# Operands moved ahead in the hand-placed front of a hybrid encoder layer

## The chip, the cores and the metric

One core of a Trainium2 chip runs the whole kernel. The metric is device time in microseconds of one execution, and the figure for a kernel is the median of its runs. TensorE (PE), VectorE (DVE), ScalarE (ACT), GpSimd (POOL) and SyncE (SP) each execute their own instructions in order; most DMAs are issued by SP, some by POOL, and they share 16 DMA engines.

## The reference, cut to what matters

One encoder layer on 1024 tokens of width 1024, float32:

```
h   = LN(x)
q, k, v, g, u, aq, ak, av = split(h @ W_in)      # 2048 columns
ret = silu(g) * groupnorm(retention(q, k, v))    # 4 heads of 64, chunks of 128
s5  = gated(C . scan(lam_bar, B u) + D u)        # 16 groups, 16 channels, 64 complex states, both directions
att = windowed GQA with ALiBi and a sink logit   # 8 heads of 64, 2 key heads, window 128
h   = LN(alpha*h + concat(ret, s5, att) @ W_out)
out = LN(alpha*h + expert_choice_swiglu(h))      # 16 experts, 128 tokens each, width 2048
```

Every float32 weight of the big products is split on the chip into a high and a low float32r part; each product is then three matmuls (high by high, high by low, low by high).

## The kernel before

`build` has three stages. `front` writes its steps into a `Plan`: `at(place, step)` gives each step a place on one axis, and `run` emits the steps sorted by place, so that the order on every engine and on SP's DMA queue is the order of the places. Places are an order, not times. After `front` a middle stage (attention scores and outputs, output projection, first layer norm, router) is emitted in a loop over half tiles and its order on the engines is chosen by the framework's scheduler. The experts, again in a written order, stream 384 pieces of weights of 1 MB.

`front` in order: eight token tiles are normalized (`Norm`: load, stats, gain, shift, turn, parts) and projected to retention keys and values (`Project`). The logarithms of the decays, `retention_consts`, are a chain of some 20 small GpSimd operations that begins with four on DVE; `decays`, on ACT, needs its end. `Norm.stats` uses GpSimd too, for one power. Then comes the S5 input product `up` (`Turned`, into `s5_input`), the input operators (`inputs`, DVE; `inputs_turn`, PE; `inputs_put`, ACT) and the output operators (`outputs`, DVE; `outputs_store`, SP: `wo_dram`; two buffers `work`). The input `u` is stored by channel to `ut_dram` and loaded by step as `U` (eight DMAs of 512-byte pieces, in the same buffer as `uT`); `s5_states_part` multiplies it with the operators, eight times, and ACT and DVE copy real and imaginary parts into `VS`. The scan (`s5_scan`, `s5_carry`) runs on DVE between other steps, and `s5_states_store` writes the states out.

`Lags` makes the short convolution blocks `m_dram`, in eight parts on PE, each with two loads (`WO`, `BX`) on SP; `Lags.store` writes one group's blocks in eight DMAs on SP. The rest of the projections runs in the order of the string `order` (`K`, `V`, `q`: attention; `g`: retention gates; `r`: retention chunks; `o`: S5 outputs). The weights of the last two query units, `W7`, are loaded at `where["r5"]`.

The output stage `Output` has four products `o0` to `o3`. Each needs a tile `MUW` of 128x4x4x128 float32 (1.05 MB: lags' blocks, `u`, two output operators; four DMAs) and two tiles `Z` of states (0.26 MB each). Their space, pool `s5o`, opens at place `O`, when the retention buffers close, so all the loads stand behind it on SP, with four buffers of `MUW`. Between them stand twelve stores of attention queries (`q_d`, 0.13 MB each) and the loads of `w_out` (`Matrix.load`, four of 1.05 MB through two `raw` buffers; `parts` splits them on ACT and DVE). `put` applies Gelu on ACT behind `parts` of the same step; `turn`, `gate` and `gated` follow and `store` writes `y2_dram`. As the last retention matrices leave, GpSimd loads the attention keys and values (3.1 MB).

The middle stage begins with `attention_consts` (distances and sinks), the loads of the layer norm's rows, `router_weights` and the first `out_proj_load`, which needs `y2_dram`.

Of the kernel before, what the change touches and what calls it, by code (L numbers as in the profile page):

```python
# [439 lines left out]
class Params:  # L440
# [4 lines left out]
    def __init__(self, K, I, pool, work):  # L445
# [12 lines left out]
        K.LT = K.s5small.tile([P, 2, 16, 16], F32, name="LT")  # L458
        K.A = K.s5small.tile([P, 2, 2, 2, 16], F32, name="A")
# [167 lines left out]
def s5_input(K, p, m, half):  # L627

    if m == 0 and half == 0:
        K.uT = K.s5w.tile([P, 2, 8, P], F32, name="uT", tag="U")  # L630
    K.nc.scalar.activation(K.uT[:, m, :, half * 64:(half + 1) * 64], p.ps.rearrange("p (k j) -> p j k", j=8), AF.Copy)


def s5_input_store(K, m):
    K.nc.sync.dma_start(K.ut_dram[m * P:(m + 1) * P], K.uT[:, m])


def s5_input_load(K):
# [74 lines left out]
class Lags:  # L713
# [35 lines left out]
    def store(self, g2):  # L749
# [5 lines left out]
        for j in range(8):  # L755
            nc.sync.dma_start(K.m_dram[g2][j * 16:(j + 1) * 16],
# [3 lines left out]
class Output:  # L760
# [17 lines left out]
    def load(self, g2, q):  # L778
# [3 lines left out]
        x = self.pool.tile([P, 4, 4, P], F32, name="MUW", bufs=4)  # L782
# [158 lines left out]
def front(K, I, pool, close):  # L941
# [35 lines left out]
    spread(4.5, 0.01, ops[4:])  # L977
# [4 lines left out]
    at(8.1, lambda: WK[0].high(1))  # L982
# [119 lines left out]
    for i, (d, q, g2) in enumerate((d, q, g2) for d in range(2) for q in range(2) for g2 in range(2)):  # L1102
# [5 lines left out]

    steps, blocks = s5_scan(K)
# [7 lines left out]
    at(e2 + 1.0, lambda: close(X["s5v"][0]))  # L1117
# [24 lines left out]
    X["out"] = Output(K, I)  # L1142
    out = X["out"]
    qs = [(g2, q) for g2 in range(2) for q in range(2)]
    for w in order:
        where[w] = s
        if w[0] in "KVq":
# [22 lines left out]
        elif w[0] == "r":  # L1170
# [12 lines left out]
            at(s + 12, c.store)  # L1183
# [13 lines left out]
    for wt, place, prev in ((W6, V0 + 15, ("K1", "V1")), (W7, where["r5"], ("q01", "q11"))):  # L1197
# [15 lines left out]
    for i, k in enumerate(qs):  # L1213
        at(O + 0.1 + 0.1 * i if i < 2 else O + 0.3 + 0.1 * i, lambda k=k: out.load(*k))
# [869 lines left out]
def build(tc, nc, I, O):  # L2084
# [193 lines left out]
```

## Time and profile before

| what | value |
|---|---|
| median of 3 runs | 1725.3 us (1721.63 to 1726.28) |
| the profiled execution, its own time | 1729.55 us |
| its span, first to last instruction | 1727.8 us |
| mean granted TensorE clock | 0.977 |
| PE busy | 1613.1 us, 93% |
| DVE busy | 1413.4 us, 82% |
| ACT busy | 1123.5 us, 65% |
| POOL busy | 203.1 us, 12% |
| moved by DMA | 512.83 MB, 297 GB/s |

Busy time is that of instructions on the engine; a busy PE is not PE at its peak, since the ends of matmuls are modelled. The clock is the granted share of 2.4 GHz. Times in rows are microseconds from the span's start.

### The profile page before, as it was taken

What the parts mean: (1) busy time and instruction counts of PE and PEld (TensorE: products, weight loads), DVE (VectorE), ACT (ScalarE), POOL (GpSimd) and SP (SyncE); (2) the same over time, 40 slices, a digit from 0 to 9 for tenths busy, and PEclk for the clock granted to TensorE, in tenths of its full rate; (3) what the DMA queues carried; (4) which work ended last, traced back from release to release, by engine and by line L of the source; (5) the groups of instructions that cost most, each with busy time, mean ns of one, the idle gap of its engine ahead of it and who ended that gap; (6) DMA issues with size and microseconds to landing.
All of it is one profiled execution on the core that took longest, in us unless ns stands there. A gap on an engine that the chain in (4) does not pass through costs nothing.

```text
span 1727.8 us, 21181 instructions
## 1 busy us (share of the span) xinstructions
PE 1613.1 (93%) x7748; PEld 1301.5 (75%) x7748; DVE 1413.4 (82%) x1721; ACT 1123.5 (65%) x1249; POOL 203.1 (12%) x235
## 2 busy tenths in 40 slices
PE   6988988489999899999999999999999999999996
PEld 4866877377777678888888888888888777777775
DVE  6886773257677998988888889898898999999995
ACT  4634353267654667777777777777777777877773
POOL 3000011001101001001011010010110313221121
PEclk9999999789999999999999999999999999999998
DMA  4564458732313899999999999999999999999993
GB/s 174 188 142 115 130 162 235 242 118 74 99 49 116 320 358 378 389 401 374 380 387 365 387 361 372 398 358 387 375 378 398 386 390 402 378 421 374 378 386 147
DMA packets 114475, 512.83 MB, mean 297 GB/s; under 512 B 13121, under 2 KB 40513, under 8 KB 63554
## 3 DMA queue, kind: packets, MB, share of 16 engines
q1 hardware_dynamic: 104242, 481.58, 73.8%
q0 software_dynamic: 10128, 29.89, 5.6%
q8 instruction: 61, 1.00, 0.2%
q14 instruction: 44, 0.36, 0.1%
HBM read 464.24 MB, written 47.19 MB: 296 GB/s over the span
## 4 chain that ended last, share of the span: by engine, by line
PE 59%; DVE 12%; DMA 11%; issue 7%; ACT 5%; SPq 3%; POOL 1%; POOLq 0%; DVEq 0%; ACTq 0%
PE gu L1753 25%; PE y L1753 12%; DVE whl L1800 6%; PE mm L74 4%; PE mm L76 4%; PE mm L75 4%; DMA zz<-acc_d 3%; DMA wraw<-in_exp_w_up 3%; DMA wraw<-in_exp_w_down 2%; ACT whl L1793 2%; PE tp L1738 2%; PE tp L1303 1%; SPq L787 1%; SPq L895 1%; DMA wraw<-in_w_out 1%
## 5 line engine op out<-in xcount | busy, mean ns | idle before, releaser
L1800 DVE TENSOR_TENSOR whl<-wraw,whl 128x2048 fp32r<-128x2048 f32 x384 | 873.5, 2289 | 101.2 <-ACT whl L1793 101.1
L1793 ACT ACTIVATE whl<-wraw 128x2048 fp32r<-128x2048 f32 x384 | 734.9, 1917 | 245.8 <-PE gu L1753 77.7
L1753 PE MATMUL gu<-whl,xT 128*128 128x512 f32 x3072 | 738.2, 397 | 0.0
L1753 PEld LDWEIGHTS gu<-whl,xT 128*128 128x128 f32 x3072 | 569.7, 188 | 123.9
L1753 PE MATMUL y<-whl,hT 128*128 128x512 f32 x1536 | 368.7, 395 | 0.7 <-ACT hT L65 0.7
L1753 PEld LDWEIGHTS y<-whl,hT 128*128 128x128 f32 x1536 | 288.7, 188 | 69.4 <-ACT hT L65 0.9
L1727 POOL DMA_INDIRECT xs<-h_d,index x15 | 41.4, 2757 | 740.8 <-PE y L1753 488.5
L74 PE MATMUL mm<-hT,whl 128*128 128x512 f32 x160 | 67.2, 420 | 4.9 <-ACT gate L354 3.3
L65 ACT ACTIVATE hT<-tp 128x512 fp32r<-128x512 f32 x80 | 46.1, 584 | 30.0 <-PE tp L1738 15.2
L76 PE MATMUL mm<-hT,whl 128*128 128x512 f32 x160 | 64.6, 403 | 0.0
L75 PE MATMUL mm<-hT,whl 128*128 128x512 f32 x160 | 64.4, 403 | 0.0
L66 DVE TENSOR_TENSOR hT<-tp,hT 128x512 fp32r<-128x512 f32 x80 | 54.2, 684 | 6.8 <-ACT hT L65 6.8
L1738 PE MATMUL tp<-ident,hid 128*128 128x128 f32 x256 | 39.6, 278 | 18.5 <-DVE hid L1835 18.5
L1738 PEld LDWEIGHTS tp<-ident,hid 128*128 128x128 f32 x256 | 31.1, 142 | 31.0 <-DVE hid L1835 24.2
L74 PE MATMUL mm<-WO,yh 128*128 128x512 f32 x128 | 52.8, 412 | 1.6 <-ACT yh L65 1.5
L75 PE MATMUL mm<-WO,yh 128*128 128x512 f32 x128 | 51.3, 401 | 0.0
L1283 ACT ACTIVATE S<-S,asm 128x384 f32<-128x384 f32 (+1 forms) x64 | 36.9, 578 | 21.3 <-DVE asm L1279 21.3
L1276 DVE CUSTOM_DVE_ANT_0 S<-at,R,sink 128x384 f32<-128x384 f32 (+1 forms) x64 | 35.8, 579 | 17.7 <-PE at L1274 13.7
L76 PE MATMUL mm<-WO,yl 128*128 128x512 f32 x128 | 50.3, 402 | 0.0
L74 PE MATMUL mm<-whl,hT 128*128 128x512 f32 (+1 forms) x128 | 47.6, 372 | 1.6 <-DVE kst L889 1.2
L1835 DVE TENSOR_TENSOR hid<-hid,gu 128x512 f32<-128x512 f32 x64 | 43.6, 681 | 1.8 <-PE gu L1753 1.8
L76 PE MATMUL mm<-whl,hT 128*128 128x512 f32 (+1 forms) x128 | 44.5, 347 | 0.0
(432 smaller groups left out, 1815.2 us busy)
## 6 DMA issues: line engine op xcount, KB each, us to landing
wraw<-in_exp_w_gate SPq DMA_DIRECT2D x128, 1024.0 KB, 8.0
wraw<-in_exp_w_up SPq DMA_DIRECT2D x128, 1024.0 KB, 8.0
wraw<-in_exp_w_down SPq DMA_DIRECT2D x128, 1024.0 KB, 7.8
wraw<-in_w_in SPq DMA_DIRECT2D x8, 1024.0 KB, 7.2
x<-in_x SPq DMA_DIRECT2D x8, 512.0 KB, 4.5
h_d<-x SPq DMA_DIRECT2D x8, 512.0 KB, 3.1
q_d<-kst SPq DMA_DIRECT2D x32, 128.0 KB, 3.2
qs<-q_d POOLq DMA_DIRECT2D x16, 256.0 KB, 3.4
```

The lines of the kernel that those rows point to most:

```text
L65: nc.scalar.activation(hi, src, AF.Copy)
L66: eng.tensor_tensor(lo, src, hi.bitcast(F32), OP.subtract)
L74: nc.tensor.matmul(ps, a[0], b[0], start=start, stop=False)
L75: nc.tensor.matmul(ps, a[0], b[1], start=False, stop=False)
L76: nc.tensor.matmul(ps, a[1], b[0], start=False, stop=stop)
L1283: nc.scalar.activation(S[g][:, :W], S[g][:, :W], AF.Exp, bias=nm[:, g:g + 1], accum_out=rs[:, g:g + 1])
L1727: nc.gpsimd.indirect_dma_start(out=xs, out_offset=None, in_=K.h1_dram, in_offset=bass.IndirectOffsetOnAxis(ap=K.index[:, e:e + 1], axis=0))
L1738: K.nc.tensor.transpose(pt[:, c, :], src[:, (c0 + c) * P:(c0 + c + 1) * P], K.ident)
L1753: nc.tensor.matmul(ps, a[s][c], u[:, t, i * w:(i + 1) * w], start=first and id(ps) not in began, stop=last and left[id(ps)] == 0)
L1793: self.K.nc.scalar.activation(u[:, 0, :], self.raw[k1].rearrange("p a b -> p (a b)"), AF.Copy)
L1800: self.K.nc.vector.tensor_tensor(u[:, 1, :], raw, u[:, 0, :].bitcast(F32), OP.subtract)
L1835: at(self.after, q, 3, lambda: nc.vector.tensor_tensor(self.h[q], self.h[q], self.pg[q][1], OP.mult))
```

## The change

The start: the decay logits are the first load; the GpSimd chain (`ops[4:]`) moves behind the second tile's statistics; the second tile's gain and shift move ahead of the second weight unit's split, and half of the first tile's product ahead of the second tile's turn. The `inputs_turn` steps are spread, the first earlier, the others later. `uT` becomes a tile of its own and is stored by step straight to `u_dram` (eight stores of 64 KB for each half `m`), `U` is read back in two DMAs, `ut_dram` and the store of `U` go; the state parts run half by half. The copies into `VS` write in order and read PSUM with a step of 16 elements, instead of the reverse. The lags' blocks are stored from GpSimd's queue. `W7` is loaded some 50 places earlier. As the scan's space closes, two new pools open in it: `early` (attention's constants, the router's operands) and `s5m` (the first two `MUW` and the first `Z` pair), and the router's weights are made there. `s5o` keeps two `MUW` buffers. The first two loads of `w_out` move ahead by 4.6 places, some stores by 2 places, and the first two expert weights are issued inside the middle loop, at its step 9.

```diff
@@ Params.__init__
+        K.uT = pool.tile([P, 2, 8, P], F32, name="uT")
@@ s5_input_store, s5_input_load
-    K.nc.sync.dma_start(K.ut_dram[m * P:(m + 1) * P], K.uT[:, m])
-def s5_input_load(K):
-    K.U = K.s5w.tile([P, 16, P], F32, name="U", tag="U")
-    src = K.ut_dram.rearrange("(g c) j k -> j c g k", c=16)
-    for j in range(8):
-        K.nc.sync.dma_start(K.U[j * 16:(j + 1) * 16], src[j])
+    dst = K.u_dram.rearrange("(j c) g k -> g c j k", j=8)
+    for g in range(8):
+        K.nc.sync.dma_start(dst[m * 8 + g], K.uT[g * 16:(g + 1) * 16, m])
+def s5_input_load(K, m):
+    K.nc.sync.dma_start(K.U[:, m * 8:m * 8 + 8], K.u_dram[:, m * 8:m * 8 + 8])
@@ s5_states_part
-        dst = K.VS[g2 * 64:(g2 + 1) * 64, ri, :, d * 8 + q * 4:d * 8 + q * 4 + 4, :].rearrange("p r q b -> p q b r")
-        src = src if d == 0 else src[:, :, ::-1]
-        src = src.rearrange("p q (b r) -> p q b r", r=16)
+        dst = K.VS[g2 * 64:(g2 + 1) * 64, ri, :, d * 8 + q * 4:d * 8 + q * 4 + 4, :]
+        src = (src if d == 0 else src[:, :, ::-1]).rearrange("p q (b r) -> p r q b", r=16)
@@ Lags.store
-            nc.sync.dma_start(K.m_dram[g2][j * 16:(j + 1) * 16],
+            nc.gpsimd.dma_start(K.m_dram[g2][j * 16:(j + 1) * 16],
@@ front
+    ops, decays = retention_consts(K, I)
     rows.load_shift()
...
-    spread(4.5, 0.01, ops[4:])
...
-    at(10.0, lambda: WK[0].low(1))
-    at(10.1, lambda: WK[1].high(0))
...
-    at(11.0, norm[1].stats)
+    at(10.0, lambda: WK[0].high(1))
+    at(10.1, lambda: WK[0].low(1))
+    at(10.2, norm[1].stats)
+    spread(10.3, 0.01, ops[4:])
+    at(11.0, norm[1].gain)
+    at(11.1, norm[1].shift)
+    at(11.2, lambda: WK[1].high(0))
...
+    at(11.6, lambda: proj[0].part(0, 4))
...
-        s = max(s, B + 5.0) + 4.0
+        s = B + 6.3 + i * 3.7
...
-    at(E0 + 4.7, lambda: s5_input_load(K))
+    at(B + 20.0, lambda: s5_input_load(K, 0))
+    at(E0 + 6.0, lambda: s5_input_load(K, 1))
...
-    at(E0 + 14.0, lambda: nc.sync.dma_start(K.u_dram, K.U))
...
-    for i, (d, q, g2) in enumerate((d, q, g2) for d in range(2) for q in range(2) for g2 in range(2)):
+    for i, (d, q, g2) in enumerate((d, q, g2) for q in range(2) for d in range(2) for g2 in range(2)):
...
-    at(e2 + 1.0, lambda: close(X["s5v"][0]))
+    def early_space():
+        close(X["s5v"][0])
+        X["early"] = pool("early")
+        attention_consts(K, I, X["early"][1])
+        router_load(K, I, X["early"][1])
+        X["s5m"] = pool("s5m")
+        for i in range(2):
+            out.load(*qs[i], X["s5m"][1])
+    at(e2 + 1.0, early_space)
+    at(e2 + 7.0, lambda: out.states(*qs[0], X["s5m"][1]))
+    at(e2 + 9.0, lambda: router_weights(K))
...
-                at(s + 2.3, lambda w=w, u=u, half=half: attention_query(K, X[w], u, half))
+                at(s + 1.8, lambda w=w, u=u, half=half: attention_query(K, X[w], u, half))
...
-    for wt, place, prev in ((W6, V0 + 15, ("K1", "V1")), (W7, where["r5"], ("q01", "q11"))):
+    for wt, place, prev in ((W6, V0 + 15, ("K1", "V1")), (W7, V0 + 21, ("q01", "q11"))):
...
-        at(O + 0.1 + 0.1 * i if i < 2 else O + 0.3 + 0.1 * i, lambda k=k: out.load(*k))
-        at(max(e2 + 5.0, O + 0.31) + 0.01 * i if i < 2 else where[f"o{i - 2}"] + 3.1, lambda k=k: out.states(*k))
+        if i > 1:
+            at(O + 0.01 * i, lambda k=k: out.load(*k))
+        if i:
+            at(O + 0.1 + 0.01 * i if i < 3 else where["o1"] + 3.1, lambda k=k: out.states(*k))
...
-        at(where["q30"] + i if i < 2 else where[f"o{i - 1}"] + 0.5, lambda i=i: X["mat"].load(2 * i))
+        at(where["q20"] + 1 + i if i < 2 else where[f"o{i - 1}"] + 0.5, lambda i=i: X["mat"].load(2 * i))
@@ build
-    attention_consts(K, I)
-    router_weights(K, I)
+        if i == 9:
+            X.load(0)
+            X.load(1)
```

## Rows read from the trace of the kernel before

**Rows 1.** Busy time by stretch: span, engines, granted clock, DMA share, GB/s.

```profile
125.00:152.00 27.00, 19.46 (x107) 16.08 (x106) 22.75 (x63) 9.98 (x11) 0.74 (x8) 0.87 0.51 132
...
152.00:180.00 28.00, 24.38 (x144) 18.66 (x144) 14.65 (x37) 10.65 (x18) 0.00 (x0) 0.94 0.57 135
...
180.00:246.00 66.00, 65.42 (x431) 57.66 (x430) 54.59 (x159) 31.61 (x66) 6.97 (x6) 1.00 0.48 124
...
246.00:277.00 31.00, 26.55 (x149) 22.59 (x148) 11.87 (x44) 12.37 (x26) 3.04 (x3) 0.94 0.61 192
...
290.20:328.50 38.30, 16.59 (x105) 15.37 (x103) 9.18 (x9) 11.96 (x15) 5.85 (x12) 0.73 1.08 317
...
355.50:546.00 190.50, 181.85 (x950) 142.31 (x951) 132.76 (x368) 124.83 (x312) 17.23 (x49) 0.97 0.23 75
...
546.00:1280.00 734.00, 724.57 (x3360) 586.89 (x3360) 660.08 (x558) 533.09 (x377) 52.97 (x31) 1.00 0.96 370
```

**Rows 2.** Waits of PE, first 600 us: for whom, total us, times, longest.

```profile
PE mm L807 <- DMA Z<-s_d: 15.5, 1, 15.5
...
PE at L734 <- DMA BX<-bx_d: 3.6, 1, 3.6
...
PE mm L74 <- ACT gate L354: 3.7, 2, 3.3
...
PE tp L599 <- DVE work L593: 1.9, 1, 1.9
```

**Rows 3.** Start, in order of time, four engines: start, us, what, idle before.

```profile
7.95 0.21 ACT L247 ACTIVATE rsmall<-rsmall 128x8 f32<-128x8 f32 x1 [5.88 <-DMA rsmall<-in_ret_theta]
...
12.57 1.29 POOL L254 TENSOR_SCALAR rsmall<-rsmall 128x8 f32<-128x8 f32 x1
...
15.09 0.27 POOL L257 TENSOR_SCALAR rsmall<-rsmall 128x8 f32<-128x8 f32 x1
...
17.11 3.49 DVE L130 TENSOR_TENSOR whl<-wraw,whl 128x1024 fp32r<-128x1024 f32 x3
...
23.95 0.21 ACT L266 ACTIVATE w<-w 128x8 f32<-128x8 f32 x1 [5.28 <-POOL w L262]
...
24.48 1.28 DVE L158 SCALAR_TENSOR_TENSOR x<-x,l0rs,bb 128x1024 f32<-128x1024 f32 x1 [1.05 <-POOL l0rs L152]
...
27.03 0.60 ACT L65 ACTIVATE hT<-tp 128x512 fp32r<-128x512 f32 x1 [2.56 <-PE tp L167]
```

**Rows 4.** S5 inputs and states, in order of time, four engines.

```profile
114.22 0.60 ACT L631 ACTIVATE uT<-mm 128x512 f32<-128x512 f32 x1 [4.41 <-PE mm L76]
...
115.24 1.36 DVE L615 TENSOR_TENSOR work<-C,PD 128x1152 f32<-128x1152 f32 x1 [2.13 <-DMA wo_d<-work]
...
118.49 3.78 SPq L643 DMA_DIRECT2D U<-ut_d  x8
...
129.87 2.05 PE L650 MATMUL at<-U,win 128*128 128x128 f32 x8 [4.69 <-DMA wo_d<-work]
...
133.04 1.05 DVE L660 COPY VS<-at 64x512 f32<-64x512 f32 x1 [0.29 <-ACT VS L658]
```

**Rows 5.** Lags' stores on SP and the last weight split on ACT.

```profile
165.05 6.14 SPq L756 DMA_DIRECT2D m_d<-KC  x8
...
251.67 1.06 ACT L125 ACTIVATE whl<-wraw 128x1024 fp32r<-128x1024 f32 x1 [6.95 <-DMA wraw<-in_w_in]
```

**Rows 6.** Output stage and what follows, in order of time.

```profile
281.20 0.43 SPq L783 DMA_DIRECT2D MUW<-m_d  x1
...
325.97 2.00 ACT L65 ACTIVATE WO<-wraw 128x1024 fp32r<-128x1024 f32 x2 [1.75 <-DMA wraw<-in_w_out]
...
344.04 0.46 POOL L1249 IOTA S<- 128x384 f32 x1 [31.30 <-DMA y_d<-YO]
...
346.60 0.99 SPq L1321 DMA_DIRECT2D y<-y_d  x2
...
352.07 3.59 PE L1373 MATMUL sm<-rwg,ones 128*128 128x32 f32 x16 [2.03 <-DMA y<-y_d]
```

More of the change, by code (lines that the diff above doesn't have):

```diff
@@ L776, in bias, with load @@
         self.K.nc.vector.tensor_scalar(self.hb, self.bg, 0.5, None, op0=OP.mult)
-    def load(self, g2, q):
+    def load(self, g2, q, pool=None):
         K, nc = self.K, self.K.nc
         gs = slice(q * 4, q * 4 + 4)
-        x = self.pool.tile([P, 4, 4, P], F32, name="MUW", bufs=4)
+        x = (pool or self.pool).tile([P, 4, 4, P], F32, name="MUW", bufs=2)
         nc.sync.dma_start(x[:, 0], K.m_dram[g2][:, gs])
@@ L788, in load, with states @@
         self.x[g2, q] = x
-    def states(self, g2, q):
-        K, nc, pool = self.K, self.K.nc, self.pool
+    def states(self, g2, q, pool=None):
+        K, nc = self.K, self.K.nc
         Z = []
         for d in range(2):
-            z = pool.tile([P, 4, P + 1], F32, name=f"Z{d}", bufs=2)
+            z = (pool or self.pool).tile([P, 4, P + 1], F32, name=f"Z{d}", bufs=1 if pool else 2)
             nc.gpsimd.memset(z[:, :, (0 if d == 0 else P):(1 if d == 0 else P + 1)], 0.0)
@@ L1003, in front @@
         p = proj[t]
-        at(s, lambda p=p: p.part(0, 3))
-        at(s + 2.3, lambda p=p: p.part(3, 6))
-        at(s + 6.2, lambda p=p: p.part(6, 8))
+        if t:
+            at(s, lambda p=p: p.part(0, 3))
+            at(s + 2.3, lambda p=p: p.part(3, 6))
+        at(s + 6.2, lambda p=p, c=6 if t else 4: p.part(c, 8))
         at(s + T + 0.05, p.rows)
@@ L1061, in windows @@
         K.win = [K.s5w.tile([P, 8, 2, 2, 64], F32, name=f"win{d}") for d in range(2)]
+        K.U = K.s5w.tile([P, 16, P], F32, name="U")
     at(B + 6.1, windows)
@@ L1106, in front @@
     at(V0 - 1.0, lambda: close(X["s5w"][0]))
+    out = Output(K, I)
+    qs = [(g2, q) for g2 in range(2) for q in range(2)]
     steps, blocks = s5_scan(K)
@@ L1141, in front @@
     where = {}
-    X["out"] = Output(K, I)
-    out = X["out"]
-    qs = [(g2, q) for g2 in range(2) for q in range(2)]
     for w in order:
@@ L1182, in front @@
             at(s + 9, c.turn)
-            at(s + 12, c.store)
+            at(s + (12 if c.t == NT - 1 else 14), c.store)
         else:
@@ L1242, in attention_keys, with attention_consts @@
         nc.gpsimd.dma_start(K.AV[:, :, half * 4:half * 4 + 4, :], K.v_dram[half])
-def attention_consts(K, I):
-    nc, cp = K.nc, K.at2
+def attention_consts(K, I, cp):
+    nc = K.nc
     K.R = cp.tile([P, 3 * P], F32, name="R")
-    rel = [cp.tile([P, 3 * P], F32, name="S", bufs=12) for _ in range(2)]
+    rel = [K.ast.tile([P, 3 * P], F32, name="rel", tag="q2", bufs=3) for _ in range(2)]
     nc.gpsimd.iota(rel[0], pattern=[[1, 3 * P]], base=-P, channel_multiplier=-1, allow_small_or_imprecise_dtypes=True)
@@ L1366, in router_weights @@
     K.rw = pool.tile([P, 2, KC, E], F32, name="rwg")
-    ones = pool.tile([P, P], F32, name="ones")
-    nc.gpsimd.memset(ones, 1.0)
-    ps = K.psm.tile([P, 2, E], F32, name="sm")
+    K.ones = pool.tile([P, P], F32, name="ones")
+    nc.gpsimd.memset(K.ones, 1.0)
+    K.rsum = pool.tile([P, 2, E], F32, name="rsum")
+    K.router = rw, gb
+def router_weights(K):
+    nc, (rw, gb) = K.nc, K.router
     for i in range(2):
         nc.vector.tensor_tensor(K.rw[:, i], rw, gb[:, i, :, None].to_broadcast([P, KC, E]), OP.mult)
+    ps = K.psm.tile([P, 2, E], F32, name="sm")
     for c in range(KC):
-        nc.tensor.matmul(ps, ones, K.rw[:, :, c, :], start=(c == 0), stop=(c == KC - 1))
-    K.rsum = pool.tile([P, 2, E], F32, name="rsum")
+        nc.tensor.matmul(ps, K.ones, K.rw[:, :, c, :], start=(c == 0), stop=(c == KC - 1))
     nc.vector.tensor_copy(K.rsum, ps)
@@ L2137, in build @@
     with tc.manual_schedule(engines={T.PE, T.Activation, T.DVE, T.Pool, T.SP}):
-        c_ast = front(K, I, pool, close)
+        c_ast, c_early = front(K, I, pool, close)
     c_kv, K.kv = pool("kv", side="right")
@@ L2153, in build @@
     nc.sync.dma_start(K.b1, bcast(I["ln1_b"], D))
-    router_weights(K, I)
+    X = K.X = Experts(K, I, O)
+    K.next_raw = lambda k: (K.raw if k < 4 or (k - 4) % 5 > 2 else K.raw2).tile([P, 2, 1024], F32, name="wraw")
     c_tk, K.tk = pool("tk")
@@ L2182, in build @@
     K.next_hl = lambda k: hl[k % 6]
-    K.next_raw = lambda k: (K.raw if k < 4 or (k - 4) % 5 > 2 else K.raw2).tile([P, 2, 1024], F32, name="wraw")
-    X = K.X = Experts(K, I, O)
-    X.load(0)
-    X.load(1)
     K.psums = c_sm, c_po, c_pa, c_pt, c_ps
     halves, pt, psums = last_tile(K, I, O, pool, close)
-    close(c_tk, c_op, c_ast, c_s5s, c_hy)
+    close(c_tk, c_op, c_early, c_ast, c_s5s, c_hy)
     c_hlb, hlb = pool("hlb", bufs=3)
```

28 lines of the change are left out of this document (12 added, 16 removed).

## The prediction

> **What bounds the kernel now.** I read the stretches first [rows 1]. The experts, 734 us of the stretch from 546 us on, keep PE busy for 724.57 us at full clock: nothing that the change touches is left there, so time won or lost ahead of them should reach the end unchanged. The middle stage is nearly as full (181.85 of 190.5 us). From 180 to 246 us the front is full too (65.42 of 66 us). The room lies in four stretches of the front: 7.5 us without PE work between 125 and 152 us, 3.6 between 152 and 180, 4.4 between 246 and 277, and 21.7 between 290.2 and 328.5 us, where the clock is 0.73 and the DMA share 1.08. Second I read for whom PE waits [rows 2]. The list names what ends the pauses: the state tiles `Z` of the output stage (15.5 us), the retention gate's copy on ACT (3.7, the longest 3.3), the lags' operand `BX` (3.6), and an input operator (1.9). Third I followed each stretch in time [rows 3 to 6]; there the S5 state product shows a DMA wait of 4.69 us [rows 4]. So the bound is PE wherever it is fed, and DMAs or a queue where it isn't; a removed PE wait counts in full unless something else is late next. What the clock costs after a pause I take from its mean: at 0.94 over 28 us, at most 0.06 x 28 = 1.7 us.
>
> **The start.** Four DVE steps of the decay constants wait for the logits until 7.95 us, and GpSimd's chain of 21 steps holds ACT's `decays` until 23.95 and DVE's second tile by 1.05 us [rows 3]. With the logits first and the chain last, both waits go, and so do two weight splits ahead of the tile (half of what is left of 17.11 to 20.6). But the chain now begins only after the second tile's power, by my layout of DVE's steps near 18.4 us (17 to 20), and `decays` still stands on ACT ahead of that tile's copies into `hT`, which ran at 27.03. The chain's length is 11.3 us before; a step takes 0.27 us, but 1.29 where DVE holds it up [rows 3]. With three of 21 held up, at 1.25, and eighteen at 0.3 with their gaps, it is about 9.3: it ends near 27.7, `decays` at 28.3, and the copies start 1.2 us later than now. PE has more of the first product behind it by then, but DVE, which starts on the third tile only after these copies, hands the delay on. I take +1.2 us; bounds: -3 (the chain ends by 24) to +4 (chain as long as before, from 20).
>
> **Input operators.** The second pair of turns waited 1.9 us for DVE [rows 2], which had waited for the first turns. The first now comes some 3 places earlier, the others later, so DVE starts sooner and PE meets finished tiles: -1.9, and about -1 for the clock: -3 (0 to -4).
>
> **u, the states and the lags.** `U` took eight DMAs of 128 KB of 512-byte pieces, issued from 118.49 and felt by PE until 129.87, where its 4.69 us end: some 11 us for 1 MB [rows 4]. (The wait is booked on `wo_d`, which lands together with the last of them.) Afterwards the first four products need only the half stored long before, and the other half is stored in eight pieces of 64 KB, by the same rate 5.5 us, then read back in long rows; it is there by the fifth product. So PE's wait goes. What is late next is DVE: its first copy into `VS` at 133.04 had waited only 0.29 us [rows 4], so products ahead of it only fill two PSUM buffers. And the eight stores stand on SP ahead of the second `wo_d` pair, which then starts 3.5 us later, and the last `outputs` on DVE needs its buffer: the first such pair already cost DVE 2.13 us [rows 4]. I lay 3 us of that on DVE. For it the copies get shorter: the trace has a copy with a step on the PSUM side, `uT`, of 0.60 us for the same 512 columns, against 1.05 with a step on the SBUF side [rows 4]. Eight of them on DVE save 8 x 0.4 = 3.2 us, the two products ahead some 2 more. Together -2 (bounds -8, if `wo_d` is in time, to +3).
> The Trainium skill ("SBUF — State Buffer", section "Door 1: The DMA port swizzle (why `[64,N]` ≈ `[32,N]`)") says that PSUM is read in lines of 8 bytes and that steps beyond a line slow an access. The row of `uT`, with a step of 32 bytes, shows no such cost on ACT; no row has it on DVE. By the rule the 3.2 us would not come, and this term would be +1.
> The blocks' eight DMAs held SP for 6.14 us from 165.05 [rows 5], with the last `BX` behind them; on GpSimd's queue they no longer do: -3.6 and -1.2 of the clock's 1.7 [rows 1, 2], -4.8 (-3 to -5.3). GpSimd has nothing else then.
>
> **W7.** ACT waited 6.95 us for it until 251.67 [rows 5], with the last states' copy and the gate's behind it, and PE 3.3 us for the gate [rows 2]. Loaded 50 places earlier it is there: -3.3, and -1.7 of the clock's 1.9 (0.06 x 31): -5 (-3 to -6). Into the same stretch come the router's 16 matmuls, 3.59 us in the slow stretch at 352.07 [rows 6], half of that at full clock: +1.8; the DVE steps beside them fit into its idle time.
>
> **The output stage.** From 281.20 to 325.97 us, when the last piece of `w_out` is there and `put` of `o3` may follow [rows 6], the loads and stores are 4.2 MB of `MUW`, 2.1 of `Z`, 3.1 of keys and values, 1.6 of queries stored and 0.5 loaded, 2.1 of `w_out`: 13.6 MB, which at 317 GB/s [rows 1] take 43 us. So this stretch is bound by bytes, and the named wait for `Z` is only where it shows. Two `MUW` and one `Z` pair, 2.6 MB, now come before it, in a stretch at 192 GB/s [rows 1]: 8.3 us. The first product starts at once, 2 us more. I take -10.5. Lower bound -5: SP still puts the other `MUW`, `Z` and all twelve query stores ahead of `w_out`. Upper bound -19: if those stores don't matter, `w_out` follows its buffers, which two splits of 2.0 us on ACT and the products between them free some 10 us after the first product, so near 300; with 3 MB still under way it lands 9 us later, 17 sooner than now, and the first product's 2 us come on top.
>
> **Into the middle.** Behind `y2_dram`, landed by 344.04, stood GpSimd's distances, DVE's four steps, six other loads ahead of the last `y` pair issued at 346.60, and the router's 3.59 us on PE [rows 6]. Three of the loads (1.4 us), the distances and the router go: -4 (-1.4 to -7). The expert weights issued in the loop are needed far later.
>
> **Sum.** +1.2 -3 -2 -4.8 -5 +1.8 -10.5 -4 = -26.3 us. The profiled execution took 1729.55 us itself, 1.75 around its span of 1727.8: 1703.2. It is 4.25 us above the median of the runs shown, so the median should come out at 1699.
>
> **Rivals.** (1) The new queues cost nothing and `w_out` goes by its buffers: U -8, output stage -19, start -1: -26.3 -6 -8.5 -2.2 = -43, 1682. For it: DMAs spread in time also land faster. Against: the share of 1.08 [rows 1]. Chance 0.14. (2) New waits eat half of it: the start +4, U +3, and the lags' blocks late. GpSimd's steps grow from 0.27 to 1.29 us where DVE works [rows 3]; sixteen DMA issues stretched like that take 20 us instead of 5, the `raw` buffers they read come free late, and the next weights stall ACT and PE as `W7` did, for another 3 to 7 us. -26.3 +2.8 +5 +5 = -13.5, 1712. Chance 0.11. The Trainium skill ("SBUF — State Buffer", section "SBUF: two separate sides") states that lock, for the descriptors of a DMA issued by GpSimd too, 3.1 us in place of 0.62; the slow GpSimd rows agree, no run here shows it for a DMA among DVE work. (3) The scan on DVE becomes the bound and swallows the front's gains but not the output stage's: DVE has 54.59 of 66 us between 180 and 246 [rows 1], too little: -14.5 +1.8, 1713, chance 0.05, counted as faster. (4) Slower: the middle stage's order is the scheduler's, and its beginning changes. It holds PE at 181.85 of 190.5 us [rows 1]; an order that leaves PE idle one fifth of the stage costs 38 us and ends at 1737; from 26 us of idle on it decides. Chance 0.05. (5) A mixture that ends within the noise: 0.03.
>
> **Chances.** Forecast 0.62. A difference under 0.3%, 5.2 us, can't be told from none here. Faster by more 0.92, within 0.03, slower 0.05. The range reaches from rival 1 to rivals 2 and 3, 1682 to 1713.
>
> **What would show it.** Right: `at` after `U` without a DMA wait and DVE's copies at 0.6 to 0.7 us; no wait for `BX`, none for the gate near `W7`; the first product directly behind the last query unit; the last `w_out` some 10 us sooner after it; no router matmuls at the middle's beginning. Wrong: PE waiting for `hT` near 29 us beyond 2 us, DVE waiting for `wo_d` longer than 4 us, ACT waiting for `w_in` near 185 us, SP standing at `MUW` loads with query stores behind, or a middle stage longer than 190 us. The largest doubt is the output stage: if bytes don't bind, its term is twice mine.

## The result, and the profile after

The changed kernel takes 1711.07 us in the median of 10 runs, the kernel before 1726.53 beside it: a ratio of 0.99 with a 95% interval of 0.9881 to 0.9918, so 14 to 21 us faster. One execution of 2276 us, and one of 3809 us of e8 below, stand outside; without them the medians are 1710.5 and, for e8, 1706.9, which changes no verdict. The forecast was 1699 with a range of 1682 to 1713: the direction held, the range at its upper end, and of the 26.3 us of the sum some 15 to 19 came. The profiled execution of the changed kernel took 1706.64 us, its span is 1704.9.

How the gain builds up shows when the same step is looked up in both traces and its shift is set against the sum of the prediction's terms up to there:

| step | before | after | shift | forecast up to there |
|---|---|---|---|---|
| ACT's copies of the second tile into `hT` | 27.03 | 27.46 | +0.4 | +1.2 |
| first lag product | 150.97 | 147.06 | -3.9 | -3.8 |
| first retention chunk's output | 186.56 | 177.28 | -9.3 | -8.6 |
| output of the last retention chunk but one (`r6`, its last head) | 252.11 | 244.58 | -7.5 | -8.6 |
| last retention chunk's output (`r7`) | 264.09 | 257.92 | -6.2 | -11.8 |
| first load of `MUW` at place `O` | 281.20 | 275.06 | -6.1 | -11.8 |
| last `put` (`o3`) | 327.88 | 313.92 | -14.0 | -22.3 |
| first matmul on `w_out` | 355.47 | 335.70 | -19.8 | -26.3 |
| first expert product | 568.80 | 550.17 | -18.6 | -26.3 |

To `r6` the sum is right within 1.1 us. Then two steps go wrong: 3.2 us forecast between `r6` and the opening of the output stage turn into a loss of 1.4, all of it ahead of `r7`, and the output stage itself gives 7.8 instead of 10.5.

The expert stage behind the last line can't be used for a verdict: over the fourteen profiled executions of this study, none of which touches its work, it lasted 1153.0 to 1162.2 us. The pair shown happens to have 1159.0 before and 1154.7 after, which is why their spans lie 22.9 us apart and the medians 15.5. I therefore judge terms by the steps of the front, and kernels by medians.

The list of PE's waits in the changed kernel (whom it waited for: total us, times, longest), against [rows 2]:

```profile
PE mm L804 <- issue: 13.5, 1, 13.5
...
PE at L648 <- DVE VS L657: 7.1, 2, 6.4
...
PE mm L74 <- ACT yh L65: 3.2, 3, 2.2
PE mm L74 <- ACT hT L65: 3.1, 1, 3.1
...
PE mm L74 <- DVE kst L886: 2.4, 2, 1.2
PE sm L1417 <- ACT rt L1407: 2.1, 2, 1.6
PE tp L867 <- ACT va L860: 2.0, 1, 2.0
...
PE sm L1394 <- DVE rwg L1391: 1.7, 1, 1.7
...
PE tp L417 <- DVE ro L411: 0.7, 1, 0.7
```

The waits of [rows 2] for `BX` and the input operator are gone, that for the gate has shrunk to 0.5 us and that for `Z` from 15.5 to 13.5 (its row names only the issue; L804 is the product that needs `Z`, whose last two transfers were issued at 300.38 us, 8 us before the wait ended). But the states now wait 7.1 us for DVE (`VS`), where they waited 4.7 for a DMA and 2.3 for DVE, and behind `r6` stand two new short waits for DVE (`ro`, `rwg`). The waits for `kst` are old; the list of the kernel before has them as

```profile
PE mm L74 <- DVE kst L889: 2.8, 2, 1.6
```

The stretches of the changed kernel (start:end, length, busy us of PE, its weight loads, DVE, ACT, POOL, granted clock, DMA share, GB/s), against [rows 1]:

```profile
251.00:256.50 5.50, 5.50 (x25) 4.77 (x26) 0.69 (x3) 1.56 (x5) 0.75 (x1) 0.69 1.11 320
...
275.06:313.92 38.86, 22.02 (x134) 19.75 (x133) 10.38 (x12) 12.13 (x15) 5.57 (x10) 0.78 1.04 305
...
416.00:426.00 10.00, 8.45 (x45) 7.32 (x44) 6.27 (x14) 8.50 (x22) 0.00 (x0) 0.70 0.39 130
...
456.00:466.00 10.00, 9.76 (x41) 7.69 (x42) 6.63 (x17) 4.68 (x10) 0.00 (x0) 0.83 0.00 0
```

And the rows in order of time that answer to [rows 3 to 6] (start, us, what, idle before and what ended it):

```profile
27.03 0.40 ACT L268 ACTIVATE dec<-lg 64x4 f32<-64x4 f32 x2
27.46 1.08 ACT L65 ACTIVATE hT<-tp 128x512 fp32r<-128x512 f32 x2
...
130.58 0.69 DVE L657 COPY VS<-at 64x512 f32<-64x512 f32 x1
...
161.77 4.51 POOL L753 DMA_DIRECT2D m_d<-KC  x8 [32.43 <-DVE sc L669]
...
182.32 1.06 ACT L125 ACTIVATE whl<-wraw 128x1024 fp32r<-128x1024 f32 x1 [4.25 <-DMA wraw<-in_w_in]
...
244.18 0.42 DVE L1264 TENSOR_SCALAR rel<-rel 128x384 f32<-128x384 f32 x1 [1.64 <-POOL rel L1263]
...
251.00 2.02 PE L1394 MATMUL sm<-rwg,ones 128*128 128x32 f32 x16 [1.73 <-DVE rwg L1391]
...
257.92 0.33 PE L385 MATMUL sm<-kv,sT 128*128 128x64 f32 x2
...
277.17 0.17 DVE L773 TENSOR_SCALAR hb<-bg 128x2 f32<-128x2 f32 x1 [10.07 <-DMA bg<-in_ssm_b_glu]
...
278.05 0.50 PE L74 MATMUL mm<-hT,whl 128*128 128x512 f32 x1 [1.23 <-DVE kst L886]
...
284.82 13.47 SPq L892 DMA_DIRECT2D q_d<-kst  x12
...
299.70 0.35 SPq L904 DMA_DIRECT2D wraw<-in_w_out  x1
...
307.49 2.00 ACT L65 ACTIVATE WO<-wraw 128x1024 fp32r<-128x1024 f32 x2 [15.32 <-DMA wraw<-in_w_out]
```

`decays` stands on ACT just ahead of the second tile's copies, as laid out in the prediction. The copies into `VS` take 0.69 us on DVE instead of 1.05 [rows 4]. GpSimd issues the lags' eight stores in 4.51 us. The twelve query stores hold SP for 13.5 us, and the third piece of `w_out` is issued behind them; ACT waits for it until 307.49, against 325.97 for the last piece before [rows 6].

The kernel before has, between `r6` and its output stage, the gate's wait, `r7`, and the same halving of the bias (`hb`) with PE waiting for `kst` behind it:

```profile
256.64 0.51 PE L74 MATMUL mm<-hT,whl 128*128 128x512 f32 x1 [3.27 <-ACT gate L354]
...
264.09 0.33 PE L385 MATMUL sm<-kv,sT 128*128 128x64 f32 x2
...
283.71 0.17 DVE L776 TENSOR_SCALAR hb<-bg 128x2 f32<-128x2 f32 x1 [10.43 <-DMA MUW<-m_d]
...
284.59 0.50 PE L74 MATMUL mm<-hT,whl 128*128 128x512 f32 x1 [1.59 <-DVE kst L889]
```

### The profile page after: what moved, and what is told of

It is laid out like the page before. It is cut to its first block, busy times and chain, and to the rows that moved or that the text cites. A ratio compares the mean times of both kernels' runs of the same rounds, so it can differ in the third digit from the quotient of the medians.

```text
span 1704.9 us, 21204 instructions
## 1 busy us (share of the span) xinstructions
PE 1612.2 (95%) x7748; PEld 1302.1 (76%) x7748; DVE 1409.3 (83%) x1721; ACT 1120.3 (66%) x1249; POOL 208.0 (12%) x251
## 4 chain that ended last, share of the span: by engine, by line
PE 64%; DVE 11%; DMA 10%; issue 7%; ACT 5%; POOL 1%; SPq 1%; POOLq 0%; DVEq 0%; ACTq 0%
PE gu L1773 28%; PE y L1773 14%; DVE whl L1820 5%; PE mm L74 4%; PE mm L75 4%; PE mm L76 4%; DMA wraw<-in_exp_w_down 3%; DMA zz<-acc_d 2%; ACT whl L1813 2%; PE tp L1758 2%; DMA wraw<-in_exp_w_up 1%; PE tp L1317 1%; DMA q_d<-kst 1%; ACT S L1297 1%; PE sm L1417 1%
## 5 line engine op out<-in xcount | busy, mean ns | idle before, releaser
L66 DVE TENSOR_TENSOR hT<-tp,hT 128x512 fp32r<-128x512 f32 x80 | 54.0, 683 | 12.7 <-ACT hT L65 12.7
L74 PE MATMUL mm<-whl,hT 128*128 128x512 f32 (+1 forms) x128 | 48.2, 376 | 4.8 <-ACT hT L65 3.1
L75 PE MATMUL mm<-whl,hT 128*128 128x512 f32 (+1 forms) x128 | 45.1, 352 | 0.2 <-DVE whl L130 0.2
L76 PE MATMUL mm<-whl,hT 128*128 128x512 f32 (+1 forms) x128 | 45.0, 351 | 0.0
```

The lines of the kernel that those rows point to most:

```text
L66: eng.tensor_tensor(lo, src, hi.bitcast(F32), OP.subtract)
L74: nc.tensor.matmul(ps, a[0], b[0], start=start, stop=False)
L75: nc.tensor.matmul(ps, a[0], b[1], start=False, stop=False)
L76: nc.tensor.matmul(ps, a[1], b[0], start=False, stop=stop)
```

## The experiments

All medians are of runs beside the kernel before, which took 1726.8 to 1727.2 us there. The intervals are about 0.25% to either side, some 4 us, so two medians less than some 6 us apart are not told from each other (4 times the root of 2, an estimate); the steps of the traces are finer, but they are those of one execution. The third column is the difference to 1711.07.

| run | median us | to the changed | ratio to before, 95% interval | opening to last put, us | first expert product |
|---|---|---|---|---|---|
| the changed kernel | 1711.07 | | 0.99 (0.9881 to 0.9918) | 38.9 | 550.2 |
| e1 query stores on GpSimd | 1705.79 | -5.3 | 0.9882 (0.986 to 0.9904) | 36.0 | 544.3 |
| e2 query stores behind `w_out` | 1698.5 | -12.6 | 0.9839 (0.9814 to 0.9864) | 31.9 | 540.3 |
| e3 router later | 1700.77 | -10.3 | 0.9854 (0.9828 to 0.9881) | 38.7 | 540.8 |
| e4 splits behind puts | 1701.79 | -9.3 | 0.9861 (0.9836 to 0.9887) | 38.9 | 539.7 |
| e5 router and bias later | 1700.0 | -11.1 | 0.9856 (0.983 to 0.9882) | 39.9 | 543.4 |
| e6 `W7` late | 1714.02 | +3.0 | 0.9917 (0.989 to 0.9944) | 39.2 | 554.8 |
| e7 state copies in the old order | 1711.09 | 0.0 | 0.9899 (0.9876 to 0.9922) | 39.2 | 552.5 |
| e8 state copies on ACT | 1708.03 | -3.0 | 0.9886 (0.986 to 0.9912) | 39.2 | 546.0 |
| e9 lags' blocks on SP | 1712.54 | +1.5 | 0.9917 (0.9889 to 0.9946) | 39.1 | 551.8 |
| e10 e2 and e4 | 1696.79 | -14.3 | 0.9826 (0.9802 to 0.9851) | 31.8 | 535.8 |
| e11 e10 and e5 | 1689.44 | -21.6 | 0.9778 (0.9754 to 0.9803) | 29.4 | 525.2 |
| e12 e11 and e8 | 1681.58 | -29.5 | 0.9739 (0.9715 to 0.9763) | 29.0 | 521.6 |

"Opening" is the first `MUW` load at place `O`.

**The output stage: bytes or SP's order (e1, e2).**

```diff
@@ e1, attention_query
-            K.nc.sync.dma_start(K.q_dram[half][h // 4][r * 64:(r + 1) * 64, :, h % 4, :],
+            e = K.nc.gpsimd if u > 1 else K.nc.sync
+            e.dma_start(K.q_dram[half][h // 4][r * 64:(r + 1) * 64, :, h % 4, :],
@@ e2: the stores of q30, q21, q31 leave attention_query
+    for w in ("q30", "q21", "q31"):
+        at(where["o2"] + 0.6, lambda w=w: query_store(K, X[w][0], int(w[1]), int(w[2])))
```

> The changed kernel, with the query stores of the last four units on GpSimd's queue instead of SP's; bytes and all else as they are. In the changed kernel twelve such stores hold SP from 284.8 to 298.3 us, and the third piece of w_out is issued behind them at 299.7, though its buffer is free near 288. Theory A (SP's order sets the output stage): the third piece is issued near 288 to 290, ACT's third split starts near 298 in place of 307.5, the last put comes 8 to 10 us sooner than 313.9, and the time falls by 7 to 10 us. Theory B (bytes, as the prediction had it): the same bytes move at 319 GB/s before the last piece has landed; it is issued sooner but lands at most 2 us sooner, and the time stays within 2 us.

> The changed kernel, with the query stores of the last three units still on SP, but behind the loads of w_out. Theory A (order): as in the run before, last put 8 to 10 us sooner. Theory B (bytes): the 1.6 MB of these stores leave the stretch ahead of the last piece, 1.6 MB / 319 GB/s = 4.9 us, so the last put comes 4 to 5 us sooner and the time falls by 4 to 5. A tells both runs alike; B tells this one from the run before by 5 us.

The stretch from the opening to the last put, first in the kernel before, then in e1 and in e2 (columns as above):

```profile
281.20:327.88 46.68, 24.00 (x136) 21.13 (x134) 10.04 (x11) 12.03 (x14) 5.85 (x12) 0.78 1.07 308
```

```profile
274.19:310.18 35.99, 25.01 (x134) 22.30 (x133) 10.30 (x11) 12.12 (x14) 12.58 (x22) 0.81 1.07 343
```

```profile
274.82:306.74 31.92, 22.03 (x134) 19.78 (x133) 10.36 (x11) 12.13 (x15) 4.71 (x9) 0.85 1.12 323
```

In e1 the third piece was issued at 287.0, 12.7 us sooner, but landed only at 300.5, 7.0 us sooner, and the last put came 3.7 us sooner (of which 0.9 stood before the opening). Order alone is not it. The whole stretch keeps the DMA engines at a share of 1.04 to 1.12, and length times rate gives the bytes: 46.68 us x 308 GB/s = 14.4 MB before, 38.86 x 305 = 11.9 in the changed kernel, 31.92 x 323 = 10.3 in e2. The first difference, 2.5 MB, is what was loaded ahead (2.6), the second, 1.5 MB, is the three units' stores (1.6). So bytes go furthest in setting it, as the prediction had it. But e2 doesn't part bytes from order quite: its last put came 7.2 us sooner, between the forecasts of its two theories, and without the stores ahead of it the last `Z` also went out 9.3 us sooner (291.1). In e1 that `Z` went out 5.9 us sooner (294.5) with the bytes left in, and the stretch is 2.9 us shorter. Neither theory had e1's gain: about the same bytes moved at 343 GB/s instead of 305. Why the rate rises with the stores on GpSimd's queue was not tried. Of e2's 12.6 us in the median the trace shows 9.9 at the first expert product.

**Between `r6` and the first output product (e3, e5, e6).**

```diff
@@ e3, and with the last two lines e5
-    at(e2 + 9.0, lambda: router_weights(K))
+    at(where["o2"] + 0.1, lambda: router_weights(K))
-        out.bias()
+    at(where["o0"] + 0.2, out.bias)
@@ e6
-    for wt, place, prev in ((W6, V0 + 15, ("K1", "V1")), (W7, V0 + 21, ("q01", "q11"))):
+    for wt, place, prev in ((W6, V0 + 15, ("K1", "V1")), (W7, where["r5"], ("q01", "q11"))):
```

> The changed kernel, with the router's two products on DVE, its 16 matmuls and their copy moved from the stretch behind the last retention chunk into the output stage, where PE stands idle for 13.5 us. Theory A (the router in that stretch ate what W7's early load gave): from the last retention chunk to the first output product 39.1 us become 33.5 to 36 (matmuls 2.0, wait for their operand 1.7, half clock from 251 to 256.5 at 0.69 another 1.7). Whether that reaches the end depends on the output stage: if SP's order sets it, everything behind moves with it, 3 to 5 us; if bytes set it, the first product comes sooner but the last put by at most 2 us. Rival: the length of the stretch is PE's own work, 39 becomes 37 and no less.

> The run with the router's products moved into the output stage, and with the halving of the gate's bias on DVE moved there too (behind the first output product). In that run PE still needed 38.3 us from the last retention chunk to the first output product, because a wait of 2.9 us for the queries' second part on DVE, which stood 10 us behind the bias's load, took the place of the router's. Theory A (a row of small waits on DVE took W7's gain, one behind the other): 38.3 becomes 35 to 36.5, the last put and the time 1.5 to 3 us sooner than in that run (308.4 and 1700.8). Theory B (PE's own work and its half clock set the stretch): 37.5 or more, and the time within 1.5 us of that run.

> The changed kernel, with W7 loaded at the old place (the sixth retention chunk) and the router's products where the change put them. Theory A (the early load is worth the 5 us of the prediction, and the router cost the stretch as much): the stretch from the last retention chunk to the first output product grows from 39.1 to 43 or 44 us and the time by 4 to 5 us. Theory B (the router's wait now stands in the same place, so W7 could come 4 us later and nobody would wait longer): at most 40.5 us and at most 1.5 us of time.

The chunk that these expectations call the last is `r6`, the last but one: the 39.1 us begin at 244.58. `r7` comes one query unit later, and the stretch must be parted there (us):

| from, to | before | changed | e3 | e5 | e6 |
|---|---|---|---|---|---|
| `r6` to `r7` | 12.0 | 13.3 | 8.0 | 7.9 | 20.0 |
| `r7` to the first output product | 26.1 | 25.8 | 30.3 | 24.2 | 25.8 |
| together | 38.1 | 39.1 | 38.3 | 32.1 | 45.8 |

Ahead of `r7` the router's products cost 5.3 us (13.3 against 8.0 in e3), as e3's theory A had added up (2.0, 1.7 and 1.7). The early load of `W7` is worth 4.0 us there without them (12.0 before against 8.0), and 6.7 beside them (20.0 in e6 against 13.3, more than e6's theory A; its first expert product came 4.6 us later, while its median, 3.0 up, tells nothing). So one edit ate the other. Yet e3's total of 33.5 to 36 was missed, since behind `r7` it lost 4.5 us at the old wait for `kst` behind the bias. That halving of the bias is no part of the change; with it moved as well, e5 has neither loss.

How, the granted clock shows. In the changed kernel its mean is 0.69 from 251.0 to 256.5 us, behind PE's waits for `ro` and `rwg`. In e3 the router's products are gone, the clock stays full there, and falls at the next pause instead, of 2.9 us, for `kst` behind the bias:

```profile
250.76 0.33 PE L385 MATMUL sm<-kv,sT 128*128 128x64 f32 x2
...
272.56 0.80 PE L74 MATMUL mm<-hT,whl 128*128 128x512 f32 x1 [2.90 <-DVE kst L886]
```

```profile
254.00:260.00 6.00, 6.00 (x29) 4.91 (x28) 2.81 (x13) 2.26 (x6) 1.01 (x1) 1.00 1.12 326
...
270.00:276.00 6.00, 3.44 (x8) 2.77 (x9) 1.48 (x3) 0.44 (x1) 0.00 (x0) 0.66 0.88 251
276.00:281.03 5.03, 5.03 (x17) 3.93 (x17) 0.00 (x0) 0.00 (x0) 0.00 (x0) 0.73 1.19 298
```

In e5 it never falls, and PE, but for 0.6 us at `ro`, has work all the time up to the first output product:

```profile
263.00:270.00 7.00, 7.00 (x33) 5.75 (x32) 0.75 (x1) 0.96 (x2) 0.00 (x0) 1.00 0.89 311
270.00:277.37 7.37, 7.37 (x34) 6.02 (x34) 0.83 (x2) 0.69 (x1) 0.20 (x4) 1.00 0.73 205
```

And in e6, where ACT waits for `W7`, the gate and the router wait one behind the other, and the clock stands at 0.50 for 12 us:

```profile
250.00:256.00 6.00, 2.96 (x12) 1.86 (x10) 3.02 (x16) 1.84 (x6) 1.17 (x1) 0.50 0.99 271
256.00:262.00 6.00, 6.00 (x20) 5.15 (x20) 0.69 (x3) 1.57 (x5) 0.00 (x0) 0.50 0.90 255
```

My expectation for e5 was wrong in that stretch, which gave more than theory A (32.1 for 35 to 36.5), and beyond it: its last put came 3.0 us later than e3's, and its median is the same. Of the 3.0 us, 2.5 stand ahead of `r6` already, where both run the same steps: from the first to the third retention chunk PE took 23.3 to 26.0 us in the changed kernel and its variants with the lags' stores on GpSimd (see the lags below). The other 0.5, and all that e5 won up to the first product, went in the output stage. The loads of the output stage start at the opening (275.1 in the changed kernel, 269.7 in e3, 271.5 in e5), and with the bytes unchanged and the query stores on SP opening to last put takes 38.7 to 39.9 us in all of e3 to e9. A first product that starts sooner finds the same bytes ahead of it.

**ACT's order in the output stage (e4).**

```diff
-        at(where[f"o{i}"] + 0.4, lambda i=i: X["mat"].parts(2 * i))
+        at(where[f"o{i}"] + 0.4 if i < 2 else G + 11.0 + 0.1 * i, lambda i=i: X["mat"].parts(2 * i))
```

> The changed kernel, with the last two splits of w_out on ACT and DVE behind the last puts and gates of the output stage (they stand ahead of the put of o2 and o3 now, and ACT waits 15.3 us for the third piece's landing at 307.4). Theory A (the pieces of w_out hold the output stage only through ACT's order; the products need just Z): the put of o2 comes near 296, that of o3 near 306 (its Z is issued at 300.4), the last gated output near 316 in place of 325.7, the first matmul on w_out 5 to 9 us sooner than 335.7; time down by 5 to 9 us. Theory B (bytes: Z of o3 and the start of the middle stage wait for the same DMAs): the last put at 311 or later, time within 3 us.

The put of `o2` came at 293.9, but the last put at 313.7, where it was, and the first matmul on `w_out` at 339.1, 3.4 us later: theory A falls, the last product waits for its `Z`. These are the rows of GpSimd, ACT and SP in e4:

```profile
297.38 1.09 POOL L1279 DMA_DIRECT2D qs<-q_d  x2 [9.23 <-DMA q_d<-kst]
298.45 0.16 POOL L792 MEMSET Z<- 128x4 f32 x2
...
293.93 0.60 ACT L808 ACTIVATE YG<-mm 128x512 f32<-128x512 f32 x1 [2.08 <-PE mm L804]
313.68 0.60 ACT L808 ACTIVATE YG<-mm 128x512 f32<-128x512 f32 x1 [19.16 <-PE mm L804]
...
299.89 1.78 SPq L793 DMA_DIRECT2D Z<-s_d  x2
```

The edge column of that `Z` is cleared on GpSimd behind a query load, which waits for the query stores; so `Z` too stands behind them, on another queue. Yet the median fell by 9.3 us, against theory B too, and all of it came in the middle stage, which none of my theories had. From the last gated output to the first expert product it took 225.5 us in the changed kernel, 215.3 in e4, and 216.1 to 216.5 in e10 to e12, which have this edit; 221.3 to 226.2 in the eight others. In the changed kernel a pause of 1.55 us at 419.1 and one of 2.24 at 456.2 stand in the stretches with a clock of 0.70 and 0.83 shown above. The two pauses are 3.8 us, and the clock's loss is 0.30 x 10 + 0.17 x 10 = 4.7 (an estimate from these rows): 8.5 of the 10.2 us between the two kernels. In e4 the stage runs at full clock from 346 us to its end:

```profile
346.00:539.73 193.73, 188.29 (x1039) 149.66 (x1038) 145.31 (x390) 122.98 (x293) 23.32 (x59) 1.00 0.26 88
```

The stage's order is the scheduler's, and it came out differently. Why this order has shorter pauses I did not try.

**The states (e7, e8).**

```diff
@@ e7
-        dst = K.VS[g2 * 64:(g2 + 1) * 64, ri, :, d * 8 + q * 4:d * 8 + q * 4 + 4, :]
-        src = (src if d == 0 else src[:, :, ::-1]).rearrange("p q (b r) -> p r q b", r=16)
+        dst = K.VS[g2 * 64:(g2 + 1) * 64, ri, :, d * 8 + q * 4:d * 8 + q * 4 + 4, :].rearrange("p r q b -> p q b r")
+        src = src if d == 0 else src[:, :, ::-1]
+        src = src.rearrange("p q (b r) -> p q b r", r=16)
@@ e8
-        if ri == 0:
-            K.nc.scalar.activation(dst, src, AF.Copy)
-        else:
-            K.nc.vector.tensor_copy(dst, src)
+        K.nc.scalar.activation(dst, src, AF.Copy)
```

> The changed kernel, with the sixteen copies of the state products written as before (step on the SBUF side). Theory A (DVE sets the end of the states, and each of its eight copies takes 1.05 us again in place of 0.69): the first scan step comes 2.5 to 4 us later than 146.64, the last carry 2 to 4 later than 238.04, the time 2 to 4 us longer. Theory B (the copies' form is covered by PE's and ACT's steps between them): first scan step within 1 us, time within 1.5 us.

> The changed kernel, with all sixteen copies of the state products on ACT (eight stand on DVE now, 0.69 us each; ACT stood idle 4.4, 5.8, 2.1, 4.3 and 1.7 us between its own). Theory A (DVE's queue is what PE waited for in the states, 7.1 us): PE's wait for DVE goes, DVE is free of 8 x 0.7 = 5.6 us, the first scan step comes 3 to 5 us sooner than 146.64, the time falls by 2 to 4 us. Theory B (the operators and the second half of U set the pace, and DVE only shows the wait): PE waits for ACT or a DMA in its place, the first scan step within 1.5 us.

With the old order DVE's copies take 1.02 to 1.07 us again, yet the first scan step comes only 1.5 us later and the last carry 1.7, and 0.5 of it stand ahead of the states (last copy into `uT` at 110.57 for 110.08); the time doesn't show it. This lies between my two theories: three of the eight copies stand behind waits for ACT (1.30, 1.60 and 0.40 us in the changed kernel), which cover part of the difference. With all copies on ACT the first scan step comes 5.4 us sooner, the last carry 6.9 and the last put 5.0, so DVE was what held the states; in the time, some 3 us less, that isn't told from none. PE's wait is now one for ACT, of 3.0 us in place of 7.1:

```profile
PE at L648 <- ACT VS L654: 3.0, 1, 3.0
```

**The lags' queue (e9).**

```diff
-            nc.gpsimd.dma_start(K.m_dram[g2][j * 16:(j + 1) * 16],
+            nc.sync.dma_start(K.m_dram[g2][j * 16:(j + 1) * 16],
```

> The changed kernel, with the sixteen stores of the lags' blocks on SP again. Theory A (the queue was worth the 4.8 us of the prediction): the eighth lag product comes 3.5 to 5 us later than in the changed kernel (167.1), PE waits 3 to 4 us for BX again, the first retention chunk's output moves from 177.3 to 181 or later, and the time grows by 3 to 5 us. Theory B (the earlier states alone let BX be in time, the queue does nothing): the eighth lag product within 1.5 us and the time within 1.5 us.

```profile
169.73 1.87 PE L731 MATMUL at<-WO,BX 128*16 128x128 f32 x8 [3.54 <-DMA BX<-bx_d]
...
160.15 6.06 SPq L753 DMA_DIRECT2D m_d<-KC  x8
```

The 3.5 us for `BX` are back behind 6.06 us of SP, and the first retention chunk's output comes at 182.3 instead of 177.3: theory A in the front. (The eighth lag product comes only 2.6 us later than 167.1, since the first came 1.0 sooner, at 146.1.) At `r6` 3.4 of the 5.0 are left. The median moved only by 1.5, which tells nothing; in the trace the last put is 3.9 us later and the first expert product 1.6, so the middle stage covered most of it in that execution.

**Together (e10 to e12).**

> Two of the runs together: the query stores of the last three units behind w_out's loads, and the last two splits behind the puts and gates. With the stores alone the third put still waited for the third piece (296.8) and the last for the fourth (304.5). Theory A (with both the puts go by Z, which was issued at 291.1 in that run): the last put comes at 299 to 302 in place of 306.7, the first matmul on w_out 2 to 5 us sooner than 328.4, the time falls to 1690 to 1696. Theory B (bytes: w_out itself is then what the first matmul waits for, and its splits stand behind the gates): the first matmul on w_out not sooner than 328, the time within 2 us of the better of the two (1698.5), unless the middle stage keeps the clock at full as it did with the splits behind (then 1690).

> The run before, with the router's products and the halving of the bias moved into the output stage too. Those moves made the stretch ahead of the first output product 7.0 us shorter, but the output stage gave 3.7 of them back, being bound by bytes. Theory A (with 1.6 MB of stores out of the way the stretch is kept): last put 4 to 6 us sooner than in the run before, time 3 to 5 us less. Theory B (the bytes still take it back): last put at most 2 us sooner, time within 2 us.

> The run before, with all sixteen copies of the state products on ACT, which alone brought the first scan step 5.4 us and the last put 5.0 us forward. Theory A (the gain of the states passes through a front that PE sets): last put 4 to 5 us sooner than in the run before, the time 3 to 5 us less, near 1685. Theory B (the bytes of the output stage take it back): last put at most 2 us sooner.

The edits are those shown. e10 went by theory B: the last put at 308.2, the first matmul on `w_out` at 334.0, and the time that of e2 within 2 us. Its middle stage was as short as e4's, for which that theory had 1690; the trace has the first expert product 4.6 us sooner than e2's, the median shows 1.7. In e11, with 1.6 MB less in the stretch, the router and bias moves were kept in full: last put 9.8 us sooner than in e10 (1.4 of them ahead of `r6`), time 7.4 less, more than I had expected. e12 gave 3.7 more at the last put, below its 4 to 5, and 7.9 of time, above its 3 to 5; of these the trace shows 3.6 at the first expert product. e12 is 29.5 us faster than the changed kernel and faster than e2 and e4, whose edits it joins. Its stretch from `r6` to the first output product, and from there to the last put:

```profile
239.41:271.50 32.09, 31.47 (x156) 25.88 (x156) 10.74 (x36) 8.83 (x22) 2.50 (x7) 1.00 0.91 267
271.50:294.60 23.10, 15.94 (x119) 15.42 (x118) 5.98 (x8) 7.54 (x10) 4.54 (x8) 0.85 1.17 360
```

## Why the prediction was right, and where its sizes were off

- **Start, inputs, states.** Right together, by luck: -3.9 at the first lag product, forecast -3.8, but from terms that missed to either side. The start cost 0.4 instead of 1.2. Start and inputs gave 4.1 by the last copy into `uT` (114.22 to 110.08; forecast -1.8), and the states then +0.2 (forecast -2). That DVE is late next there was right, and e8 shows it. That eight shorter copies give 3.2 us was too much: e7 gives them 1.0 to 1.5. The Trainium skill ("SBUF — State Buffer", section "Door 1: The DMA port swizzle (why `[64,N]` ≈ `[32,N]`)") gives PSUM lines of 8 bytes, where steps slow matmuls, and SBUF lines of 16 bytes, where each access that crosses to a new line pays. The trace shows no cost of the step in PSUM for a copy: with a step of 64 bytes there it took 0.69 us on DVE, as much as a copy of 512 columns out of PSUM in order (the row below). With steps of 512 bytes on the SBUF side, which the prediction left out of that rule, it took 1.02 to 1.07, and that agrees.

```profile
540.25 0.69 DVE L1409 COPY rt<-tp 128x512 f32<-128x512 f32 x1
```

- **Lags.** -5.4 between the first lag product and the first retention chunk, forecast -4.8; e9 puts 5.0 at that chunk on the queue. Of it 1.8 were lost again up to `r6`, in the way of rival 2, in small. Beside the second group's stores the next weights come late: ACT waits 4.25 us for them until 182.32, 5.0 us behind the first chunk's output (3.2 before, 3.0 in e9, after waits of 2.35 and 2.2), and PE then 2.0 us for `va` on ACT. In the twelve traces with the stores on GpSimd's queue that pause of PE is 0.2 to 2.0 us, before it is 0.1, in e9 there is none.
- **W7 and the router.** Here a step failed. For `W7` "-5" came as -4.0 (12.0 to 8.0 us ahead of `r7`), but "the DVE steps beside them fit into its idle time" was wrong: DVE had the time, not the place. The router's products stood in DVE's order so that PE waited 1.7 us for them, PE waited 0.7 behind the four steps on GpSimd's distances, and behind both pauses the clock fell to a mean of 0.69. In place of +1.8 the router cost 5.3 (e3), and -3.2 became +1.4. The bias was no part of it: PE waited behind it 1.6 us before, 1.2 after.
- **The output stage.** Bound by bytes, as forecast: from opening to last put it needs 38.9 us instead of 46.7, 7.8 less, against 8.3 worked out from 2.6 MB. The "2 us more" for a first product that starts at once were wrong, because the end goes by the bytes counted from the opening (e5). The lower bound of 5 was on the right side, and rival 1 fell with e1: `w_out` doesn't go by its buffers, the third piece landed 13.4 us behind its issue.
- **Into the middle.** -5.8 between last put and first matmul on `w_out`, forecast -4.
- **Left out.** "Time won or lost ahead of them should reach the end unchanged" holds for the experts, not for the middle stage, whose length changed by up to 10 us with its scheduled order (e4); from the first matmul on `w_out` to the first expert product it took 214.5 us in the changed kernel, 213.3 before. Rival 4 named that mechanism on the losing side only; the mean clock of 0.97 over its 190.5 us [rows 1] showed the room. Rival 2's stretched GpSimd issues did not appear: the lags' stores took 0.56 us each. The Trainium skill ("SBUF — State Buffer", section "SBUF: two separate sides") gives 3.1 us for a DMA issued so beside a copy on VectorE; DVE ran only multiplies, adds and subtractions there, so no run here shows that case.
- **Signs and rivals.** Two signs of being wrong did show: PE waited 3.1 us for `hT`, until 28.11, which cost little since it had waited 4.4 us there before, and ACT waited for `w_in` near 185 us, as said. The measured 1711 lies nearer to rivals 2 and 3 (1712 and 1713) than to 1699, but neither made it: the start, `U` and the blocks were not late, and from the third to the seventh chunk PE takes 41.2 to 41.4 us in all fourteen traces, the kernel before among them, so DVE's scan sets nothing there.

Not settled: why the scheduler's order of e4 pauses less, and why e1 moved its bytes faster.

## What to carry to other kernels

Work moved into an engine's idle time is free only if nothing that the critical engine needs stands behind it in the queue: look for whom the queue serves next, not for its busy share. Where a stage is bound by bytes, count them from the first load's issue, and move bytes out of it before moving its start or its order. Price a pause of PE with the clock behind it, and look at the mean clock of a full stage before calling it full.

## What was not expected of the hardware

Short pauses of TensorE can cost more than themselves. Behind PE waits of 0.7 and 1.7 us the granted clock has a mean of 0.69 for 5.5 us in the changed kernel, and over the 11 us that begin in a pause of 2.9 us it is 0.66 to 0.73 in e3, while with a single one of 0.6 the clock stayed at 1.00 for 32 us (e5, e12). Not each pause does it: in the changed kernel the clock stayed at 1.00 around the 2.0 us for `va` (178 to 206 us) and the 1.2 for `kst` (278 to 290). The DMA engines moved 305 GB/s in the output stage with the query stores on SP, 343 with them on GpSimd's queue, at shares of 1.04 and 1.07.
